# Down products of two SwiGLUs by Strassen's scheme, with the operands formed beside gate and up and kept in DRAM

## Chip, cores and metric

The kernel runs on one core of one Trainium2 chip. The metric is device time in microseconds (us) of one execution. The engines are TensorE (PE, with its weight loads PEld), VectorE (DVE), ScalarE (ACT), GpSimd (POOL) and SyncE (SP); SP and POOL here also issue the DMA transfers.

## What is computed

A decoder layer on x of 1024 positions by 1024 features, in float32. A SwiGLU (D_FF = 2816) stands ahead of the mixing block and another behind it:

```
def swiglu(x, w_gate, w_up, w_down):
    return (jax.nn.silu(x @ w_gate) * (x @ w_up)) @ w_down

x = x + 0.5 * swiglu(rms_norm(x, ffn1_norm), ffn1_w_gate, ffn1_w_up, ffn1_w_down)
# projection, sliding-window attention and chunkwise mLSTM, gated and merged: x = x + merged @ w_out
x = x + 0.5 * swiglu(rms_norm(x, ffn2_norm), ffn2_w_gate, ffn2_w_up, ffn2_w_down)
return rms_norm(x, final_norm)
```

## The kernel before

Features lie on the 128 partitions, positions on the free axis, in two halves of 512 (`HALVES`). A float32 matmul is done as three matmuls of type float32r: each operand is split into a high and a low part, and hi x hi, hi x lo and lo x hi are summed in PSUM (`mm3`, L318 to L320). A split is one copy on ACT (`whi`, L77 or L337) and one subtraction on DVE (`wlo`, L89 or L338; L337 and L338 are `parted`, which also splits moving operands).

**Gate and up** (`gate_up`) already use Strassen's scheme (Winograd's form: 7 products and 15 sums for a 2 x 2 of blocks). The blocks are halves of the features, halves of the positions, and pairs of row tiles s and s + 11. `PRODUCTS` is the order 1, 2, 6, 7, 4, 5, 3; a product is done for gate and for up (w = 0, 1), each a `group` of 12 matmuls (L421) into one PSUM bank. Product 2 accumulates in product 1's bank, products 7 and 4 in product 6's, product 3 in product 5's; DVE adds the rest (L447 for products 6 and 7, L451 for 4, 5 and 3). The first `LEAD` = 4 pairs do products 1 and 2 ahead, while DVE still prepares the operands of the others (`mixed`); after that a round takes all 7, in the first three pairs the 5 that are left. `gated` forms silu(gate) * up with one tanh on ACT (L429) and two operations on DVE (L432, L433) and writes the result to DRAM, `gd`, with the pair's row and half. Weights are split three products ahead (`prepare`, `split`), and sums of weights are formed in place (`sum_of`, L411).

**Down** (`ffn`) is a plain product: six chunks of row tiles (`CHUNKS`: 2, then 4 each). `fetch` loads the results of a chunk back from `gd` (L534) through the ring `nsq` of 24 tiles and splits them into one of three slots; `tail` starts the first three while gate and up finish. `down` does, for an output tile d and a half, the matmuls of a chunk in one bank, and DVE adds a quarter of it to the residual tile (L567). Residual tiles X are loaded as the stage begins (`loadx`). In the last chunk each finished tile goes to `done`: in the first SwiGLU it is written out, and when the first half is complete its norm is formed (`norm`: L264 sums of squares, L307 on DVE, L308 on ACT, L310 on POOL) while PE does the other half; in the second SwiGLU the final norm is formed (`final`), the end in `QUARTERS`.

Each engine takes its instructions in the order in which the program issues them; the schedule is written by hand. `bg` holds generators, and `pump` advances each by one step behind every group. A tile that is allocated anew waits for the last use of its buffer.

## Time and profile before

| | |
|---|---|
| median of 3 runs | 2519.94 us (2517.06 to 2520.85) |
| the profiled execution | 2524.41 us, of which its span is 2522.6 |
| mean granted TensorE clock | 0.978 of full speed |
| first SwiGLU: gate and up, down | about 20 to 467 us, 467 to 720 |
| mixing | about 720 to 1810 us |
| second SwiGLU: gate and up, down | about 1810 to 2251 us, 2251 to 2510 |

Times in the rows are counted from the span's start. A busy time is the union of an engine's instructions; the granted clock (PEclk) is a share of TensorE's full 2.4 GHz, and 0.5 is its other level. A line of waits says which instruction kept an engine idle until it ended; L447 or L567 there is a line of the kernel.

### The profile page before, as it was taken

What the parts mean: (1) busy time and instruction counts of PE and PEld (TensorE: products, weight loads), DVE (VectorE), ACT (ScalarE), POOL (GpSimd) and SP (SyncE); (2) the same over time, 40 slices, a digit from 0 to 9 for tenths busy, and PEclk for the clock granted to TensorE, in tenths of its full rate; (3) what the DMA queues carried; (4) which work ended last, traced back from release to release, by engine and by line L of the source; (5) the groups of instructions that cost most, each with busy time, mean ns of one, the idle gap of its engine ahead of it and who ended that gap; (6) DMA issues with size and microseconds to landing.
All of it is one profiled execution on the core that took longest, in us unless ns stands there. A gap on an engine that the chain in (4) does not pass through costs nothing.

```text
span 2522.6 us, 29816 instructions
## 1 busy us (share of the span) xinstructions
PE 2418.4 (96%) x11370; PEld 2004.2 (79%) x11370; DVE 1557.2 (62%) x2520; ACT 874.9 (35%) x1546; POOL 241.0 (10%) x210
## 2 busy tenths in 40 slices
PE   7899999899998999999999999999889999999997
PEld 6788888688887878888777788888668888878886
DVE  6876666554468864555658944445687666665535
ACT  4323223321136642333346623332432223231203
POOL 0000000000034330000233400000000000000002
PEclk8999999999999999999999999999889999999998
DMA  4322221542241212222531122223523222245322
GB/s 171 103 84 92 75 84 63 191 143 84 76 135 59 72 61 87 77 86 84 173 104 56 49 86 86 74 82 126 170 72 105 88 88 77 78 140 159 111 59 92
DMA packets 115183, 246.08 MB, mean 98 GB/s; under 512 B 10976, under 2 KB 18272, under 8 KB 115040
## 3 DMA queue, kind: packets, MB, share of 16 engines
q1 hardware_dynamic: 112976, 243.18, 30.0%
q8 instruction: 90, 1.47, 0.2%
q0 software_dynamic: 1200, 0.79, 0.2%
q14 instruction: 53, 0.43, 0.1%
q10 hardware_dynamic: 864, 0.21, 0.0%
HBM read 207.69 MB, written 36.44 MB: 97 GB/s over the span
## 4 chain that ended last, share of the span: by engine, by line
PE 77%; DVE 14%; ACT 3%; DMA 2%; issue 2%; SPq 0%; DVEq 0%; POOL 0%; ACTq 0%
PE mm L421 30%; PE mm L318 13%; PE mm L319 13%; PE mm L320 13%; DVE P L973 1%; PE mm L834 1%; DVE PT L1012 1%; PE mm L835 1%; PE mm L836 1%; DVE wlo L89 1%; DVE P L993 1%; DVE nsq L264 1%; PE lm L1114 1%; DMA nsq<-xd 1%; PE lm L1142 1%
## 5 line engine op out<-in xcount | busy, mean ns | idle before, releaser
L318 PE MATMUL mm<-s,whi 128*128 128x512 f32 (+1 forms) x1776 | 705.4, 397 | 16.3 <-DVE nsq L567 15.4
L320 PE MATMUL mm<-s,wlo 128*128 128x512 f32 (+1 forms) x1776 | 695.6, 392 | 1.7 <-POOL wlo L89 1.5
L421 PE MATMUL mm<-s,whi 128*128 128x512 f32 x2112 | 664.6, 396 | 33.9 <-DVE nsq L447 13.3
L319 PE MATMUL mm<-s,whi 128*128 128x512 f32 (+1 forms) x1776 | 694.9, 391 | 0.0
L421 PEld LDWEIGHTS mm<-s,whi 128*128 128x128 f32 x2112 | 403.0, 191 | 123.1 <-DVE nsq L447 14.2
L421 PE MATMUL mm<-s,wlo 128*128 128x512 f32 x1056 | 416.4, 394 | 0.0
L318 PEld LDWEIGHTS mm<-s,whi 128*128 128x128 f32 x1776 | 338.2, 190 | 87.2 <-ACT whi L77 13.7
L320 PEld LDWEIGHTS mm<-s,wlo 128*128 128x128 f32 x1776 | 337.7, 190 | 74.8 <-POOL wlo L89 3.2
L319 PEld LDWEIGHTS mm<-s,whi 128*128 128x128 f32 x1776 | 338.4, 191 | 64.7
L77 ACT ACTIVATE whi<-wraw 128x1024 fp32r<-128x1024 f32 (+2 forms) x210 | 215.0, 1029 | 234.1 <-PE mm L319 109.6
L89 DVE TENSOR_TENSOR wlo<-wraw,whi 128x1024 fp32r<-128x1024 f32 (+2 forms) x188 | 227.0, 1207 | 68.9 <-ACT whi L77 68.5
L567 DVE SCALAR_TENSOR_TENSOR nsq<-mm,nsq 128x512 f32<-128x512 f32 (+1 forms) x196 | 131.5, 678 | 201.7 <-PE mm L320 169.7
L421 PEld LDWEIGHTS mm<-s,wlo 128*128 128x128 f32 x1056 | 201.9, 191 | 43.1 <-DVE wlo L338 0.8
L337 ACT ACTIVATE whi<-wr 128x1024 fp32r<-128x1024 f32 x110 | 116.2, 1058 | 208.2 <-PE mm L421 155.1
L338 DVE TENSOR_TENSOR wlo<-wr,whi 128x1024 fp32r<-128x1024 f32 x110 | 134.3, 1222 | 53.3 <-ACT whi L337 53.2
L337 ACT ACTIVATE s<-nsq 128x512 fp32r<-128x512 f32 x112 | 67.9, 626 | 170.0 <-DMA nsq<-gd 155.3
L451 DVE TENSOR_TENSOR nsq<-mm,nsq 128x512 f32<-128x512 f32 x132 | 90.9, 688 | 56.3 <-PE mm L421 55.7
L89 POOL TENSOR_TENSOR wlo<-wraw,whi 128x1024 fp32r<-128x1024 f32 x22 | 52.7, 2400 | 708.5 <-ACT whi L77 708.5
L447 DVE TENSOR_TENSOR nsq<-mm,nsq 128x512 f32<-128x512 f32 x88 | 60.6, 690 | 96.0 <-PE mm L421 96.0
L429 ACT ACTIVATE nsq<-nsq 128x512 f32<-128x512 f32 x66 | 41.8, 633 | 192.2 <-DVE nsq L451 190.2
L421 PE MATMUL mm<-nsq,whi 128*128 128x512 f32 x352 | 108.4, 389 | 0.0
L338 DVE TENSOR_TENSOR s<-nsq,s 128x512 fp32r<-128x512 f32 x112 | 76.0, 688 | 45.7 <-ACT s L337 45.4
(250 smaller groups left out, 2732.9 us busy)
## 6 DMA issues: line engine op xcount, KB each, us to landing
wraw<-win SPq DMA_DIRECT2D x84, 512.0 KB, 3.6
wr<-gu SPq DMA_DIRECT2D x74, 512.0 KB, 4.1
wraw<-dn SPq DMA_DIRECT2D x48, 512.0 KB, 3.8
...
```

The source lines that it names most:

```text
L77: self.nc.scalar.activation(hv, v, AF.Copy)
L89: (self.nc.gpsimd if self.on_pool else self.nc.vector).tensor_sub(lv, v, hv.bitcast(F32))
L318: nc.tensor.matmul(ps, hi, xh, start=first, stop=False)
L319: nc.tensor.matmul(ps, hi, xl, start=False, stop=False)
L320: nc.tensor.matmul(ps, lo, xh, start=False, stop=last)
L337: nc.scalar.activation(hi, x, AF.Copy)
L338: nc.vector.tensor_sub(lo, x, hi.bitcast(F32))
L421: nc.tensor.matmul(ps, a[:, k], op[p](k, x), start=first and k == 0 and j == 0, stop=k == 3 and j == 2, skip_group_check=not first)
L429: nc.scalar.activation(st["th"], z[0], AF.Tanh, scale=0.5)
L447: nc.vector.tensor_add(t, ps, st[s, "s1", w])
L451: nc.vector.tensor_add(z, ps, z)
L567: nc.vector.scalar_tensor_tensor(x, ps, 0.25, x, op0=OP.mult, op1=OP.add)
```

## The change

Down becomes 7 products too. The row tiles are three chunks of pairs (`DOWN`: 4, 4 and 3 pairs f and f + 11), the outputs are pairs d, d + 1 (dp = 0 to 3), the blocks of the other factor are its halves by row and by position. A step is one product of one chunk: 4 banks (dp), in each 3 matmuls per pair.

The operands of the products are sums of the four results of a pair. `paired` forms them behind the pair's last product, splits each, and writes 7 x 2 tiles to `gd` in DRAM; for the first four pairs one result is parked in DRAM (`gx`) until then. `fetch` loads a product's operands, both parts, by one transfer on POOL's queue into one of two buffers in slot 1. The weights of a chunk are loaded by four transfers (`load`) into slot 0 or 2, summed in place and split two units a step.

In gate and up each product has its own PSUM bank, apart from 2 and 3; what 7 and 4 took from the bank is added on DVE (L458 and L461 in the order below). Products 1 and 2 of the next pair stand on both sides of product 3. The factor 0.25 of the down product goes into `gated`, where a `tensor_mul` becomes a `scalar_tensor_tensor`. The slots of the mixing part are exchanged, and the final norm counts d in another order. Cut to its core:

```diff
-CHUNKS = [(0, FT % CHUNK)] + [(f, CHUNK) for f in range(FT % CHUNK, FT, CHUNK)]
+DOWN = ((0, 4), (4, 4), (8, 3))
...
         def product(s, p, w, first):
-            key = {1: "A", 2: "A", 6: "C", 7: "C", 4: "C", 5: "B", 3: "B"}[p]
+            key = {2: 1, 3: 5}.get(p, p)
...
-                nc.vector.tensor_mul(th, th, z[1])
-                nc.sync.dma_start(gd[s + S2 * m, :, half * HS:(half + 1) * HS], th)
+                nc.vector.scalar_tensor_tensor(t, t, 0.25, z[1], op0=OP.mult, op1=OP.mult)
+                if (m, half) == (0, 0) and s < LEAD:
+                    nc.sync.dma_start(gx[s], st.pop(("g", s, 0, 0)))
+
+        def paired(s):
+            if s < LEAD:
+                st["g", s, 0, 0] = t = temp(pool)
+                nc.sync.dma_start(t, gx[s])
+            (a, b), (c, d) = ([st.pop(("g", s, m, h)) for h in range(2)] for m in range(2))
+            f = nc.vector.tensor_sub
+            for p, x, sub in ((3, d, (f, d, d, b)), (2, c, (f, b, b, a)), (1, a, (nc.vector.tensor_add, a, a, d)),
+                              (7, d, (f, c, c, a)), (5, b, None), (6, a, None), (4, c, None)):
+                part = [temp(pool, R32) for _ in range(2)]
+                parted(x, *part)
+                for i in range(2):
+                    nc.sync.dma_start(gd[PRODUCTS.index(p), s, :, i], part[i].bitcast(F32))
+                yield
+                if sub:
+                    sub[0](*sub[1:])
+                    yield
...
-                key, m, half = {4: ("s1", 1, 0), 5: ("u7", 1, 1), 3: ("u6", 0, 1)}[p]
-                z = st[s, key, w]
-                nc.vector.tensor_add(z, ps, z)
+                key, to, m, half = {4: (7, 1, 1, 0), 5: (7, 7, 1, 1), 3: (6, 6, 0, 1)}[p]
+                nc.vector.tensor_add(st[s, to, w], ps, st[s, key, w])
...
+                if p == 3 and w:
+                    bg.append(paired(s))
...
+        def load(c, i):
+            s0, a = DOWN[c]
+            flat = slot(i, [16 * HS], F32)
+            for m in range(2):
+                for h in range(2):
+                    t = flat[:, (2 * m + h) * 4 * a * 128:][:, :4 * a * 128]
+                    f = FT // 2 * h + s0
+                    nc.sync.dma_start(t.rearrange("p (d x) -> p d x", d=4),
+                                      I[f"dn{n}"][m::2, :, f:f + a].rearrange("d p f c -> p d (f c)"))
+                    raw[c, m, h] = t
+
+        def fetch(i):
+            if i < len(steps):
+                c, p = steps[i]
+                s0, a = DOWN[c]
+                t = moving["buf"][:, i % 2, :a]
+                nc.gpsimd.dma_start(t, gd[PRODUCTS.index(p), s0:s0 + a].rearrange("s p i t -> p s i t"))
+                moving[i] = t
...
         def tail(p):
+            if p == 2:
+                load(0, 0)
+            elif p == 7:
+                moving["buf"] = slot(1, [2, 4, 2, HS])
+                fetch(0)
+                fetch(1)
             elif p == 5:
+                load(1, 2)
...
+        for i, (c, p) in enumerate(steps):
+            if i:
+                fetch(i + 1)
+            if i == 2:
+                for d in range(0, KT, 2):
+                    loadx(d, 1)
+            elif i in (3, 4):
+                for d in range(1, KT, 2):
+                    loadx(d, i - 3)
+            if (c, p) == (1, 1):
+                load(2, 0)
...
+            for span in spans:
+                for dp in range(4):
+                    cols = slice(span[0] % HS, span[0] % HS + span[1])
+                    ps = times(i, moving[i], dp, cols)
+                    if dp % 2 == 0 and span[0] != QUARTERS[1][0]:
+                        t = prepare()
+                    elif dp % 2 and t:
+                        sum_of(*t)
+                        t = None
+                    add = nc.vector.tensor_add
+                    if p == 1:
+                        u[dp] = temp(pool)
+                        nc.scalar.activation(u[dp], ps, AF.Copy)
+                    elif p in (6, 7):
+                        if p == 7:
+                            add(X[2 * dp][1], X[2 * dp][1], u[dp])
+                        add(u[dp], ps, u[dp])
+                    else:
+                        d, h = {2: (0, 0), 4: (1, 0), 5: (1, 1), 3: (0, 1)}[p]
+                        x = X[2 * dp + d][h]
+                        if p in (4, 5):
+                            add(x, x, u[dp])
+                        add(x[:, cols], ps, x[:, cols])
+                        if end:
+                            done(2 * dp + d, span)
+                    pump()
...
-    gd = dram.tile([FT, 128, S], F32, name="gd")
+    gd = dram.tile([len(PRODUCTS), FT // 2, 128, 2, HS], F32, name="gd")
```

Three places in the instruction order. The first is DVE in the early part of the first SwiGLU's gate and up, at the adds of products 6 and 7 of pair 0 (`mm_664` and the like are PSUM banks, `wlo_678` the low half of the weights for product 4). Before:

```order
L338 TENSOR_TENSOR wlo_678<-wr_288,whi_677 128x1024
L447 TENSOR_TENSOR nsq_681<-mm_664,nsq_305 128x512
L447 TENSOR_TENSOR nsq_710<-mm_695,nsq_320 128x512
L198 TENSOR_SCALAR bhalf_712<-binf_685 128x42
L205 CAST identr_714<-ident_74 128x128
L206 TENSOR_SCALAR lmask_716<-nsq_683 128x128
L338 TENSOR_TENSOR wlo_734<-wr_389,whi_733 128x1024
L447 TENSOR_TENSOR nsq_737<-mm_664,nsq_305 128x512
```

And of the changed kernel:

```order
L328 TENSOR_TENSOR wlo_679<-wr_289,whi_678 128x1024
L458 TENSOR_TENSOR nsq_682<-mm_665,nsq_306 128x512
L458 TENSOR_TENSOR nsq_711<-mm_696,nsq_321 128x512
L188 TENSOR_SCALAR bhalf_713<-binf_686 128x42
L195 CAST identr_715<-ident_74 128x128
L196 TENSOR_SCALAR lmask_717<-nsq_684 128x128
L328 TENSOR_TENSOR wlo_736<-wr_390,whi_735 128x1024
L458 TENSOR_TENSOR nsq_739<-mm_722,nsq_682 128x512
```

No row moved; the last one, the add of product 7, reads a bank of its own (`mm_722`), where it read product 6's (`mm_664`).

The second is DVE in a long round, from product 6 to the first add of product 4 or, in the changed kernel, of product 7. Before:

```order
L338 TENSOR_TENSOR wlo<-wr,whi 128x1024
L447 TENSOR_TENSOR nsq<-mm,nsq 128x512 x2
L338 TENSOR_TENSOR wlo<-wr,whi 128x1024
L447 TENSOR_TENSOR nsq<-mm,nsq 128x512 x2
L338 TENSOR_TENSOR wlo<-wraw,whi 128x1024
L451 TENSOR_TENSOR nsq<-mm,nsq 128x512
```

And of the changed kernel, where L444 is a sum and L328 with `nsq` a split of `paired`:

```order
L458 TENSOR_TENSOR nsq<-mm,nsq 128x512
L444 TENSOR_TENSOR nsq<-nsq 128x512
L458 TENSOR_TENSOR nsq<-mm,nsq 128x512
L328 TENSOR_TENSOR nsq<-nsq 128x512
L328 TENSOR_TENSOR wlo<-wraw,whi 128x1024
L458 TENSOR_TENSOR nsq<-mm,nsq 128x512
L444 TENSOR_TENSOR nsq<-nsq 128x512
```

Between the adds of a product there now stands one operation of `paired` for each group.

The third is POOL from the early constants to the norm ahead of the mixing part, which holds the whole first down stage. Before:

```order
L182 IOTA nsq 128x256
L274 TENSOR_TENSOR nv<-nv,mhalf 128x4
L310 TENSOR_TENSOR s_4584<-nsq,s_4584 128x512 x8
L689 MEMSET hist 128x24
L691 MEMSET C 128x1040
```

And of the changed kernel:

```order
L172 IOTA nsq 128x256
L564 DMA s_3554<-gd 128x4x1024 x14
L564 DMA s_3554<-gd 128x3x1024 x7
L264 TENSOR_TENSOR nv<-nv,mhalf 128x4
L300 TENSOR_TENSOR s_4799<-nsq,s_4799 128x512 x8
```

The 21 fetches of the down stage are POOL's only work there, ahead of the norm's.

## Rows read from the trace of the kernel before

**Rows 1.** The page: span, TensorE's busy time, its granted clock by slices, one group.

```profile
span 2522.6 us, 29816 instructions
PE 2418.4 (96%) x11370; PEld 2004.2 (79%) x11370; DVE 1557.2 (62%) x2520; ACT 874.9 (35%) x1546; POOL 241.0 (10%) x210
...
PEclk8999999999999999999999999999889999999998
...
L318 PE MATMUL mm<-s,whi 128*128 128x512 f32 (+1 forms) x1776 | 705.4, 397 | 16.3 <-DVE nsq L567 15.4
```

**Rows 2.** Busy times by stretch (first row: columns): inside gate and up, inside down.

```profile
core 0: us, PE busy (x) PEld busy (x) DVE busy (x) ACT busy (x) POOL busy (x), PEclk, DMA share, GB/s
200.00:300.00 100.00, 100.00 (x443) 82.81 (x442) 62.33 (x74) 29.01 (x34) 0.00 (x0) 1.00 0.26 85
300.00:400.00 100.00, 100.00 (x443) 82.81 (x442) 67.51 (x80) 29.87 (x36) 0.00 (x0) 1.00 0.25 82
...
520.00:660.00 140.00, 140.00 (x619) 115.93 (x618) 67.93 (x93) 28.67 (x39) 0.00 (x0) 1.00 0.30 92
```

**Rows 3.** The same by stretch: both early gate-and-up parts, both starts of down.

```profile
85.00:120.00 35.00, 28.33 (x118) 22.96 (x117) 30.96 (x56) 8.68 (x11) 0.34 (x1) 0.90 0.37 114
1870.00:1900.00 30.00, 23.32 (x91) 18.75 (x91) 23.68 (x31) 5.51 (x6) 0.00 (x0) 0.83 0.30 101
467.00:505.00 38.00, 28.90 (x118) 22.70 (x117) 21.24 (x32) 11.95 (x19) 0.00 (x0) 0.91 0.74 236
2251.00:2290.00 39.00, 32.67 (x132) 26.12 (x131) 22.97 (x35) 13.06 (x19) 0.00 (x0) 0.91 0.74 246
```

**Rows 4.** What PE waited for, whole span: us in total, times, longest.

```profile
PE mm L318 <- DVE nsq L567: 15.4, 5, 6.7
PE mm L421 <- DVE nsq L447: 13.3, 2, 6.7
```

**Rows 5.** Groups of instructions by line and shape: busy us, mean ns, idle before.

```profile
L338 DVE TENSOR_TENSOR wlo<-wr,whi 128x1024 fp32r<-128x1024 f32 x110 | 134.3, 1222 | 53.3 <-ACT whi L337 53.2
...
L451 DVE TENSOR_TENSOR nsq<-mm,nsq 128x512 f32<-128x512 f32 x132 | 90.9, 688 | 56.3 <-PE mm L421 55.7
L338 DVE TENSOR_TENSOR s<-nsq,s 128x512 fp32r<-128x512 f32 x112 | 76.0, 688 | 45.7 <-ACT s L337 45.4
...
L337 ACT ACTIVATE s<-nsq 128x512 fp32r<-128x512 f32 x112 | 67.9, 626 | 170.0 <-DMA nsq<-gd 155.3 <-DVE nsq L1368 11.0 <-DVE nsq L346 2.3
```

**Rows 6.** DMA from 10 to 20 us, SyncE's queue alone, loads at full share.

```profile
DMA packets 2130, 3.97 MB, mean 397 GB/s; under 512 B 191, under 2 KB 191, under 8 KB 2130
```

**Rows 7.** Lines L1192 and L1225, the transfers on POOL's queue (ns of issue).

```profile
L1192 POOL DMA_DIRECT2D s<-kh x2: 778/790/803, 1266.2 to 1355.5; - x2
...
DMA to landing us min/median/max: 3.4/3.7/4.0
...
L1225 POOL DMA_DIRECT2D VS<-vh x1: 766/766/766, 1265.5 to 1265.5; - x1
```

**Rows 8.** DMA: queue share from 1355 to 1361 us; GB/s from 1356.8 to 1358.6.

```profile
q0 software_dynamic: 528, 0.26, 24.1%
...
GB/s 0 0 0 0 46 23 46 23 23 68 114 148 148 148 159 171 239 216 296 319 330 330 319 341 353 319 319 319 273 250 171 103 68 68 46 23 11 0 0 0
```

**Rows 9.** Order of time, end of the first SwiGLU: start us, us, engine and line.

```profile
697.95 0.69 DVE L264 TENSOR_TENSOR nsq<-nsq 128x512 f32<-128x512 f32 x1 [0.70 <-ACT nsq L262]
...
717.60 5.92 POOL L310 TENSOR_TENSOR s<-nsq,s 128x512 fp32r<-128x512 f32 x4 [2.27 <-ACT s L308]
```

**Rows 10.** What PE waited for from 2480 to 2523 us, the longest.

```profile
PE mm L271 <- DVE nsq L264: 5.2, 1, 5.2
```

**Rows 11.** Busy times at the first two issues on POOL's queue, columns as above.

```profile
1265.50:1266.50 1.00, 1.00 (x10) 1.00 (x10) 0.00 (x0) 0.00 (x0) 1.00 (x2) 1.00 0.33 131
1355.50:1356.50 1.00, 1.00 (x7) 1.00 (x6) 0.93 (x6) 0.59 (x1) 0.79 (x2) 0.50 0.06 16
```

More of the change, by code (lines that the diff above doesn't have):

```diff
@@ L23 @@
 FT = 2816 // 128
-CHUNK = 4
 HALVES = ((0, HS), (HS, HS))
@@ L465, in behind @@
                     load(s + 1 if p == 2 else s + 2, 0, 0)
-        ahead = set(range(LEAD))
+        early = set(range(LEAD))
         for h in range(2):
@@ L480, in gate_up @@
             load(3, 0, h)
-        ahead.clear()
+        early.clear()
         yield
@@ new lines, in times @@
+        def times(i, t, dp, c):
+            key = (dp, {2: 1, 3: 5}.get(steps[i][1], steps[i][1]))
+            first = steps[i][1] not in (2, 3)
+            if first:
+                bank[key] = psum.tile([128, HS], F32, name="mm")
+            ps = bank[key][:, c]
+            hi, lo = (x[:, dp % 2] for x in parts[2 * i + dp // 2])
+            a = hi.shape[1]
+            for f in range(a):
+                for q, (wt, x) in enumerate(((hi, 0), (hi, 1), (lo, 0))):
+                    nc.tensor.matmul(ps, wt[:, f], t[:, f, x, c], start=first and f == 0 and q == 0,
+                                     stop=f == a - 1 and q == 2, skip_group_check=not first)
+            return ps
@@ L1444, in done2 @@
         else:
-            stats(pool, fa[h][:, own], x, d == 0)
+            stats(pool, fa[h][:, own], x, first)
             fa[p] = [fa[h][:, own]]
```

192 lines of the change are left out of this document (82 added, 110 removed).

## The prediction

> **What bounds the kernel now.** I read the page's first two parts, then busy times by stretch. TensorE is busy 96% of the span and its granted clock is at the full level nearly everywhere [rows 1]. Inside gate and up, and inside the down products, PE is 100% busy at clock 1.00, and neither VectorE (62 to 68% and 49%) nor ScalarE limits it [rows 2]. So a stage costs its matmuls times their pitch: 100 us for 443 matmuls and 140 us for 619 [rows 2], 0.226 us for one of 512 columns (the 397 ns that one of them lasts [rows 1] overlap its neighbours). Then I looked where PE stops. Two places in each SwiGLU matter here. At the start of the down products, 38 us hold 118 matmuls (26.7 us at that pitch) and 39 us hold 132 (29.8): 11.3 + 9.2 = 20.5 us are lost, to L567, whose residual tile and operand come late from DRAM, and to the lower clock behind the pause [rows 3, 4]. And in the early part of gate and up, product 7 stops 6.7 us for the add of product 6 (L447), which still has to read the PSUM bank into which 7 accumulates, and stands in VectorE's queue behind the preparation of the operands; 118 matmuls in 35 us and 91 in 30 lose 8.3 and 9.4 us there [rows 3, 4].
>
> **The change part by part.** All sums are against the profiled execution's 2524.4 us (span 2522.6 and 1.8 around it); it lies 4.5 us above the median 2519.9, so 4.5 come off at the end.
>
> (a) *Fewer matmuls.* Down had 22 row tiles x 8 x 2 halves x 3 = 1056 matmuls a SwiGLU, now 7 products x 4 x 11 x 3 = 924. 2 x 132 x 0.226 = **-59.7 us**, all on the path.
>
> (b) *Start of the down products.* Before, fetch and residual tiles were asked for when the stage began. Now the first weights go out after product 2 of the last round, two fetches after its product 7, i.e. three products of 24 x 0.226 = 5.4 us ahead: 16.3 us for 2 x 2.1 MB, and the second is needed 10.9 us later still. Residual tiles are needed only at the second product. I leave 1 us a SwiGLU for the seam: **-18.5 us** (bounds -20.5 and -10).
>
> (c) *Own PSUM banks.* Product 7 no longer waits for L447. What is late next is its neighbour's weight: the low half for product 4 stands one row ahead of those adds in VectorE's queue, and VectorE, behind by some 8 us there, gets to it when PE has finished 7. So 1 to 2 us of each stop stay, and since PE then runs ahead of a VectorE that has more to do (d), part comes back later. Of 17.7 us I take **-7 us** (bounds -15 and 0).
>
> (d) *Operands formed beside gate and up.* A round of 7 products is 168 matmuls, 38.0 us; VectorE is busy 62.3 + 67.5 us in 200, so 24.7 in a round [rows 2]. `paired` adds 7 splits and 4 sums of 512 columns, 11 x 0.69 = 7.6 us [rows 5]: 32.3 of 38.0, 85%, still hidden. ScalarE gets 7 x 0.63 = 4.4 on some 11. The first three rounds have 5 products, 27.1 us; VectorE has 5 weight splits (6.1), 4 sums (4.9), 10 evictions (6.9), 6 gatings (4.1) and the 7.6: 29.6 us by single durations, a tenth less back to back. It falls behind by 0 to 2.5 us a round, against weights split three products (16 us) ahead. If every split also waits for ScalarE as L338 did (45.7 us over 112, 0.41 each [rows 5]), the long rounds come to 32.3 + 14 x 0.41 = 38.0, no loss, and the short ones to 29.6 + 12 x 0.41 = 34.5, 7.4 late each: 44 us in both SwiGLUs. A VectorE that is behind finds ScalarE done, so I stay near the low end: **+4 us** (0 to 44). Writing 7 x 2 x 0.26 = 3.7 MB a round instead of 1.0 gives some 152 GB/s with the weights, where 397 was moved at full load [rows 6].
>
> (e) *Fetching the operands.* The operands were split after loading; now both halves come from DRAM: 21 fetches, 2.1 MB each (1.57 in the last chunk), through GpSimd's queue, each into the buffer that the product before last leaves. So a fetch has one product's time: 48 x 0.226 = 10.9 us (8.1 in the last chunk). Its nearest row is the 256 KB that GpSimd's queue moves into `s` (kh): 3.4 us alone [rows 7], with its packets at 319 to 353 GB/s on the plateau [rows 8]. At 335, 2.6 us are fixed and 2.1 MB take 6.3: 8.9 of 10.9, hidden; in the last chunk 7.3 of 8.1. Not hidden where SyncE's queue moves as much at once: the second chunk's weights (4.2 MB, asked for 5 us before the stage), 14 writes of the last round's operands and 16 residual tiles fall on steps 1 to 4, the third chunk's weights on 7 and 8; in the first SwiGLU the results go out during three steps of the last chunk. With both queues at 366 GB/s in all (between 335 and 397 [rows 6, 8]), a fetch beside 2.1 MB takes 2.6 + 11.5 = 14.1, 3.3 late; beside 1.05 MB 0.4 late: 3 x 3.3 + 3 x 0.4 = 11.1 a SwiGLU, and 3 x 1.7 = 5.1 in that last chunk. **+27 us** (17 at 397, 40 at 335).
>
> A rule to weigh here: the Trainium skill (DMA: Bandwidth & Descriptors, Anatomy of one DMA) fits a GpSimd-issued transfer with 2.0 us plus its bytes at 436 GB/s, an estimate of 6.8 us for 2.1 MB; the trace's 256 KB took 3.4 us where that fit gives 2.6, so it does not quite agree and the row decides. By the page's figure (e) would be about 4 us and the time 2453.
>
> (f) *Seam to the mixing part.* The first half of the residual was final 8 groups of 12 matmuls (21.7 us) before PE ended; now two steps, 16.3 us. Its norm is a chain from VectorE's last sum (at 697.95) to GpSimd's last low half (717.60 + 5.92), four of them 5.9 us [rows 9]: 25 us, of which PE now covers 5.4 less and VectorE's two adds per tile in products 4 and 5 delay the start: **+7 us** (2 to 12).
>
> (g) *End.* Before, PE waited 5.2 us there for the sums of squares [rows 10]. Now VectorE has two adds where it had one in products 4 and 5 (8 x 0.69 = 5.5 us more): **+3 us** (0 to 8). VectorE's weight splits and evictions in the down products (per step 2.4 + 1.4 + 3.5 = 7.3 of 10.9 us) cost nothing while PE and the fetch take longer.
>
> Sum: -59.7 - 18.5 - 7 + 4 + 27 + 7 + 3 = -44.2; 2524.4 - 44.2 = 2480.2, less 4.5: **2476 us**.
>
> **The rivals.** *All hidden* (the fetches cost 5 at most, the stops of (c) go by 13, the seam costs 5, end and (d) 2 each): -59.7 - 18.5 - 13 + 2 + 5 + 5 + 2 = -77.2, 2443. For it: SyncE's queue alone reached 397 GB/s; against: some 20 MB are wanted in the first 54 us of the stage, which is nearly that rate throughout. *The fetch is slow throughout* (the other side): it converts to another type on the way, and over its whole share, 24.1% of 6 us [rows 8], the 256 KB moved at 181 GB/s. At 181 a fetch takes 2.6 + 11.6 = 14.2 us, 3.3 late in 13 steps and 3.2 in 7: 65 us a SwiGLU, 131 in place of the 27: 2524.4 - 44.2 - 27 + 131 = 2584, 2580 by the median. It decides from where the 40 steps eat 71 us, 1.8 us each, a landing at 12.7 us or 208 GB/s. Against it stands the plateau, with packets of only 512 bytes. *VectorE bounds gate and up*: (d) at 44 and (c) at 0, 2523, no change. *GpSimd cannot write descriptors while VectorE works*: then every fetch starts an instruction (1.2 us) later, hidden in the plain steps, 1.2 more in the 15 contested ones: 18 us, 2494. Against: one issue took 0.77 us with VectorE idle and one 0.80 with it 93% busy [rows 7, 11]. The Trainium skill (SBUF — State Buffer, Who interferes with whom) states such a lockout for VectorE's two-port modes and excepts tensor_tensor, and the two issues agree. That the change does not drop the matmuls is excluded by the instruction order, which holds 924 of them a SwiGLU (those of 256 columns counted as halves).
>
> **How the numbers follow.** Forecast 0.54 (its own range 2455 to 2500), all hidden 0.25, slow fetch 0.10, VectorE-bound 0.08, lockout 0.03. The range leaves out the slow fetch and the worst of VectorE: 2440 to 2518. About 0.2% (5 us) is what a measurement of this kernel can tell from no change. Faster: 0.54 + 0.25 + 0.03 and a quarter of VectorE-bound, 0.84; same 0.04; slower 0.12.
>
> **What would show it.** PE's count in the down stage 7/8 of before; no wait of PE for the add of product 6; PE's waits inside the down products named to GpSimd's queue and lying at steps 1 to 4 and 7 to 8 alone (forecast), nowhere (all hidden), or in each step with about 3 us (slow fetch); median landing of a fetch 9 to 10 us, or 7, or 14. VectorE over 95% busy in gate and up with PE under 100% would be the VectorE case. I am wrong above all if the landing time of 2.1 MB is not what 256 KB let one expect.

## The result and the profile after

The changed kernel takes 2482.30 us (median of 4 runs, 2477.79 to 2483.14), the kernel before 2520.39 (4 runs, 2517.06 to 2522.57): a ratio of 0.9846 with a 95% interval of 0.9829 to 0.9863. The forecast was 2476 us with a range of 2440 to 2518. The profiled execution took 2482.01 us, its span is 2479.4: 43.2 us less than the span before, where the sum of the prediction said 44.2. By stage, from the first and last matmul of each (us):

| stage | before | after | difference |
|---|---|---|---|
| ahead of the first matmul of gate and up | 19.7 | 19.4 | -0.3 |
| gate and up, first SwiGLU | 447.4 | 453.5 | +6.1 |
| down, first, up to the first matmul of mixing | 252.4 | 229.4 | -23.0 |
| mixing | 1092.6 | 1087.8 | -4.8 |
| gate and up, second | 438.9 | 437.5 | -1.4 |
| down, second, and the end | 271.6 | 251.8 | -19.8 |

The total is close, the stages less so: the first gate and up became slower, and mixing, in which the forecast counted nothing but its seam, became faster.

The page of the changed kernel (L626 is now the matmul of down, L413 that of gate and up, L461 and L458 VectorE's sums from PSUM in gate and up, L564 the fetch):

```profile
span 2479.4 us, 30117 instructions
...
PE 2365.1 (95%) x11094; PEld 1956.3 (79%) x11094; DVE 1740.1 (70%) x2780; ACT 944.0 (38%) x1664; POOL 258.0 (10%) x246
...
s<-gd POOLq DMA_DIRECT2D x28, 2048.0 KB, 9.3
...
s<-gd POOLq DMA_DIRECT2D x14, 1536.0 KB, 6.9
```

TensorE has 53 us less work than in [rows 1] and VectorE 183 us more. The last figures of the DMA rows are the medians from issue to landing of a fetch: 9.3 and 6.9 us, where 8.9 and 7.3 were forecast. The rival of the slow fetch (14.2 us) falls with these two rows.

Busy times by stretch, columns as in [rows 2]:

```profile
85.00:120.00 35.00, 29.64 (x120) 24.05 (x119) 31.57 (x57) 9.27 (x12) 0.35 (x1) 0.90 0.43 133
...
200.00:300.00 100.00, 100.00 (x443) 82.84 (x442) 82.03 (x106) 38.36 (x54) 0.00 (x0) 1.00 0.51 166
300.00:400.00 100.00, 100.00 (x443) 82.84 (x442) 81.83 (x107) 38.64 (x54) 0.00 (x0) 1.00 0.44 144
...
460.00:500.00 40.00, 34.70 (x139) 27.81 (x138) 30.30 (x38) 14.36 (x21) 1.48 (x2) 0.92 1.08 394
1860.00:1900.00 40.00, 36.67 (x155) 29.89 (x155) 35.86 (x47) 14.14 (x18) 0.00 (x0) 0.96 0.33 112
```

In the long rounds VectorE went from 62 to 68 up to 82 us in 100, TensorE still never stops there, and the writes of the operands brought 144 to 166 GB/s (152 with the weights were forecast). From 460 us the DMA queues are full: 394 GB/s.

What TensorE waited for in the whole span (total, times, longest), and the places in order of time (start, duration; in brackets the wait ahead of it):

```profile
PE mm L261 <- DVE nsq L254: 21.5, 7, 5.3
PE mm L413 <- DVE nsq L461: 15.9, 6, 5.4
PE mm L626 <- DMA s<-gd: 12.8, 6, 3.3
```

```profile
109.79 0.77 PE L413 MATMUL mm<-nsq,whi 128*128 128x512 f32 x1 [5.36 <-DVE nsq L461]
...
465.74 0.70 PE L413 MATMUL mm<-nsq,whi 128*128 128x512 f32 x2 [3.11 <-DVE nsq L461]
...
497.00 1.11 PE L626 MATMUL mm<-s,whi 128*128 128x512 f32 x2 [2.19 <-DMA s<-gd]
...
558.23 0.87 PE L626 MATMUL mm<-s,whi 128*128 128x512 f32 x2 [3.03 <-DMA s<-gd]
...
682.81 1.44 PE L261 MATMUL mm<-mean,nsq 128*128 128x2 f32 x6 [3.72 <-DVE nsq L254]
...
2252.81 0.80 PE L626 MATMUL mm<-s,whi 128*128 128x512 f32 x1 [3.29 <-DMA s<-gd]
```

The wait for the residual tile (L567 in [rows 4]) is gone: the first down matmul follows the last of gate and up without a pause. The wait of product 7 for product 6's sum (L447) is gone too, but L461 stands in its place. A matmul whose moving operand is `nsq` belongs to product 3, and product 3 accumulates in product 5's bank, which L461 reads. The waits for an operand number three in each SwiGLU; by the count of matmuls they stand at the start of steps 3, 5 and 8 both times.

To weigh the terms I counted, from the starts of successive matmuls in the timeline, how much later than the pitch (0.2267 us per 512 columns) each came; this takes in the lower clock behind a stop. That lateness, before and after:

| place | before | after | term, forecast | term, by lateness |
|---|---|---|---|---|
| (a) 2 x 132 matmuls fewer | | | -59.7 | -59.8 |
| (b) start of down | 11.6 + 9.4 | 0 | -18.5 | -21.0 |
| (c) early stop in gate and up | 9.0 + 9.9 | 8.0 + 5.2 | -7 | -5.7 |
| (d) stops at 169, 466, 1927, 2222 us | 0 | 2.2 + 5.2 + 1.1 + 1.6 | +4 | +10.1 |
| (e) waits for an operand | 0 | 10.9 + 9.0 | +27 | +19.9 |
| (f) seam to mixing | 0.3 | 7.2 | +7 | +6.9 |
| (g) half and quarter norms, end | 8.6 + 11.6 | 6.4 + 11.5 + 11.9 | +3 | +9.6 |
| mixing | | | 0 | -4.8 |
| sum | | | -44.2 | -44.8 |

The remaining 1.6 us to the measured 43.2 lie in places below what this count resolves. The sum was right because errors of both signs met: (d) and (g) came out 6 us higher each, (e) and mixing 7 and 5 lower. That it came within 1 us is in part luck. So the experiments ask after the terms one by one.

### The profile page after: what moved, and what is told of

Read it like the earlier page. It is cut to its first block, busy times and chain, and to the rows that moved or that the text cites. A ratio compares the mean times of both kernels' runs of the same rounds, so it can differ in the third digit from the quotient of the medians.

```text
span 2479.4 us, 30117 instructions
## 1 busy us (share of the span) xinstructions
PE 2365.1 (95%) x11094; PEld 1956.3 (79%) x11094; DVE 1740.1 (70%) x2780; ACT 944.0 (38%) x1664; POOL 258.0 (10%) x246
## 4 chain that ended last, share of the span: by engine, by line
PE 51%; DVE 12%; DMA 3%; ACT 3%; issue 3%; SPq 0%; DVEq 0%; POOL 0%; ACTq 0%; POOLq 0%
PE mm L413 14%; PE mm L308 7%; PE mm L310 7%; PE mm L309 7%; PE mm L626 5%; DMA gd<-nsq 2%; DVE P L1042 1%; PE mm L903 1%; DVE PT L1081 1%; PE mm L904 1%; PE mm L905 1%; DMA s<-gd 1%; DVE P L1062 1%; DVE wlo L87 1%; PE lm L1183 1%
## 5 line engine op out<-in xcount | busy, mean ns | idle before, releaser
L413 PE MATMUL mm<-s,whi 128*128 128x512 f32 x2112 | 659.6, 393 | 19.7 <-ACT nsq L452 9.4
L413 PEld LDWEIGHTS mm<-s,whi 128*128 128x128 f32 x2112 | 400.0, 190 | 107.1 <-ACT nsq L452 11.1
L308 PE MATMUL mm<-s,whi 128*128 128x512 f32 x1056 | 423.5, 401 | 0.9 <-DVE s L1368 0.9
L310 PE MATMUL mm<-s,wlo 128*128 128x512 f32 x1056 | 415.4, 393 | 1.5 <-POOL wlo L87 1.5
L309 PE MATMUL mm<-s,whi 128*128 128x512 f32 x1056 | 414.6, 393 | 0.0
L413 PE MATMUL mm<-s,wlo 128*128 128x512 f32 x1056 | 414.2, 392 | 0.0
L626 PE MATMUL mm<-s,whi 128*128 128x512 f32 (+1 forms) x1256 | 391.4, 394 | 15.3 <-DMA s<-gd 12.8
L626 PEld LDWEIGHTS mm<-s,whi 128*128 128x128 f32 x1256 | 239.8, 193 | 66.5 <-DMA s<-gd 6.3
L626 PE MATMUL mm<-s,wlo 128*128 128x512 f32 (+1 forms) x628 | 246.2, 392 | 0.0
L413 PEld LDWEIGHTS mm<-s,wlo 128*128 128x128 f32 x1056 | 200.4, 190 | 42.7 <-DVE wlo L328 0.8
L87 DVE TENSOR_TENSOR wlo<-wraw,whi 128x1024 fp32r<-128x1024 f32 (+1 forms) x138 | 171.5, 1243 | 69.6 <-ACT whi L75 69.1
L75 ACT ACTIVATE whi<-wraw 128x1024 fp32r<-128x1024 f32 (+1 forms) x154 | 159.7, 1042 | 74.1 <-PE mm L310 23.7
L327 ACT ACTIVATE whi<-wr 128x1024 fp32r<-128x1024 f32 (+1 forms) x122 | 128.0, 1050 | 156.3 <-PE mm L413 92.8
L328 DVE TENSOR_TENSOR wlo<-wr,whi 128x1024 fp32r<-128x1024 f32 (+1 forms) x122 | 147.6, 1212 | 36.4 <-ACT whi L327 34.7
L327 ACT ACTIVATE whi<-s 128x1024 fp32r<-128x1024 f32 (+1 forms) x72 | 71.0, 986 | 238.2 <-PE mm L626 230.4
L564 POOL DMA_DIRECT2D s<-gd x42 | 31.8, 756 | 1188.5 <-DMA s<-dn 783.4
L626 PEld LDWEIGHTS mm<-s,wlo 128*128 128x128 f32 x628 | 121.1, 193 | 24.3
L328 DVE TENSOR_TENSOR nsq<-nsq 128x512 fp32r<-128x512 f32 x162 | 110.6, 686 | 31.6 <-ACT nsq L327 29.0
L413 PE MATMUL mm<-nsq,whi 128*128 128x512 f32 x352 | 113.3, 404 | 15.9 <-DVE nsq L461 15.9
## 6 DMA issues: line engine op xcount, KB each, us to landing
s<-dn SPq DMA_DIRECT2D x16, 1024.0 KB, 11.2
```

The source lines that it names most:

```text
L75: self.nc.scalar.activation(hv, v, AF.Copy)
L87: (self.nc.gpsimd if self.on_pool else self.nc.vector).tensor_sub(lv, v, hv.bitcast(F32))
L308: nc.tensor.matmul(ps, hi, xh, start=first, stop=False)
L309: nc.tensor.matmul(ps, hi, xl, start=False, stop=False)
L310: nc.tensor.matmul(ps, lo, xh, start=False, stop=last)
L327: nc.scalar.activation(hi, x, AF.Copy)
```

## The experiments

All runs in one table. Times in us; the ratio is that to the kernel before on the same chip, with its 95% interval; the stages are those of the profiled execution.

| run | median | ratio | gate/up 1 | down 1 | mixing | gate/up 2 | down 2, end |
|---|---|---|---|---|---|---|---|
| changed kernel | 2482.30 | 0.9846 (0.9829-0.9863) | 453.5 | 229.4 | 1087.8 | 437.5 | 251.8 |
| e1_nopair | 2471.08 | 0.9807 (0.9794-0.9821) | 446.2 | 232.5 | 1088.5 | 434.3 | 249.0 |
| e2_spread | 2482.04 | 0.9847 (0.9827-0.9866) | 454.7 | 232.4 | 1088.9 | 436.4 | 252.1 |
| e3_stats | 2477.88 | 0.9832 (0.9816-0.9848) | 453.6 | 225.9 | 1088.4 | 437.2 | 250.8 |
| e4_shared | 2495.53 | 0.9909 (0.9893-0.9924) | 457.9 | 234.7 | 1086.7 | 444.6 | 251.3 |
| e5_paced | 2469.76 | 0.9796 (0.9783-0.9810) | 450.5 | 224.7 | 1089.4 | 435.6 | 247.9 |
| e6_pool | 2480.70 | 0.9844 (0.9830-0.9857) | 454.4 | 231.8 | 1088.2 | 439.0 | 250.3 |
| e7_shared_nopair | 2480.92 | 0.9842 (0.9828-0.9856) | 447.0 | 235.8 | 1086.2 | 439.0 | 253.5 |
| e8_stats2 | 2475.68 | 0.9826 (0.9812-0.9840) | 448.1 | 224.3 | 1095.1 | 438.0 | 248.8 |
| e9_own3 | 2460.03 | 0.9755 (0.9742-0.9769) | 438.1 | 230.6 | 1086.2 | 430.1 | 252.3 |
| e10_all | 2449.07 | 0.9714 (0.9701-0.9727) | 440.4 | 221.0 | 1095.0 | 429.5 | 240.8 |
| e11_latefetch | 2479.55 | 0.9838 (0.9823-0.9852) | 448.8 | 228.5 | 1088.7 | 436.1 | 253.2 |
| e12_latefetch2 | 2512.36 | 0.9965 (0.9952-0.9977) | 450.2 | 250.3 | 1088.6 | 436.2 | 266.9 |

How far apart must two runs be? The gate and up of e2, e3, e5, e8, e11 and e12 is the changed kernel's, and its first one took 448.1 to 454.7 us in those profiles, mainly since the stop near 462 us lasted anything from 1.1 to 5.4 us; the first 20 us of the stage make up to 2.5 us more. The stop's length goes with what VectorE itself waited for transfers just ahead of it: 1.3 us in e8 (stop 1.1), 3.4 in the changed kernel (3.1), 5.6 in e2 (5.4). So a difference of 3 us between two medians says little, and where one matters I go by the stage.

### The added work on VectorE (e1_nopair)

```diff
-                part = [temp(pool, R32) for _ in range(2)]
-                parted(x, *part)
                 for i in range(2):
-                    nc.sync.dma_start(gd[PRODUCTS.index(p), s, :, i], part[i].bitcast(F32))
+                    nc.sync.dma_start(gd[PRODUCTS.index(p), s, :, i], x)
                 yield
                 if sub:
-                    sub[0](*sub[1:])
                     yield
```

> Left out: the splits and sums of paired (7 copies on ScalarE, 7 subtractions and 4 sums on VectorE in a round); the 14 writes to gd a round stay, of unsplit values. Compared with the changed kernel (2482.3 us, ratio 0.985). Theory 1, VectorE's queue: the stops of TensorE that are new there (at 160, 460, 1920 and 2220 us; matmuls start 2.2 + 5.2 + 1.1 + 1.6 = 10.1 us late against the pitch) go with the work: 2472 us, VectorE in 200 to 300 us back from 82 to about 62 busy. Term (d) of the prediction: 4 us, 2478. Rival, the DMA queue: the stops at the stage's end (460 and 2220) come from transfers that are late there, the 6.8 us of them stay: 2479.

11.2 us less. The stage that answers is the right one: gate and up lost 7.3 + 3.2 us. Busy times of this run in the long rounds, and its waits of TensorE for that sum (L458 in its numbering):

```profile
200.00:300.00 100.00, 100.00 (x443) 82.81 (x442) 64.71 (x75) 28.57 (x34) 0.00 (x0) 1.00 0.54 173
```

```profile
PE mm L413 <- DVE nsq L458: 8.5, 2, 5.4
```

Two of the six stops are left, those at 110 and 1866 us; the four new ones are gone although the writes stayed. So (d) comes from the added work, and is about 10 us, not 4. At the stop of 169 us VectorE is busy without a pause, 9.96 of the 10 us from 160 on. For the two at the stage's end (466 and 2222 us) its queue is not the whole: in the changed kernel VectorE itself waits for transfers just ahead of the first, from 450 to 467 us:

```profile
DVE nsq L328 <- DMA gd<-nsq: 1.8, 1, 1.8
DVE s L575 <- DMA s<-dn: 1.6, 1, 1.6
```

The first is a buffer that a write of an operand still holds, the second the down weights. In e1 there is no such wait: the buffers of the split operands and ScalarE's seven copies went with the edit. So e1 does not part VectorE's work from the full DMA queue there.

### Shared banks, with and without that work (e4_shared, e7_shared_nopair)

```diff
-            key = {2: 1, 3: 5}.get(p, p)
+            key = {2: 1, 7: 6, 4: 6, 3: 5}.get(p, p)
...
-            ps = product(s, p, w, p not in (2, 3))
+            ps = product(s, p, w, p in (1, 6, 5))
...
-                nc.vector.tensor_add(t, ps, st[s, {6: 1, 7: 6}[p], w])
+                nc.vector.tensor_add(t, ps, st[s, 1, w])
...
-                key, to, m, half = {4: (7, 1, 1, 0), 5: (7, 7, 1, 1), 3: (6, 6, 0, 1)}[p]
+                key, to, m, half = {4: (1, 1, 1, 0), 5: (7, 7, 1, 1), 3: (6, 6, 0, 1)}[p]
```

> Only the PSUM banks of gate and up are undone: products 7 and 4 accumulate in product 6's bank, as in the kernel before. Compared with the changed kernel (2482.3 us). Theory 1, a stop that moved: TensorE stops again at product 7 for 6.7 us and no longer at product 3 for 5.4 and 3.3; lateness 9.0 + 9.9 in place of 8.0 + 5.2, 5.7 us: 2488. Term (c) of the prediction: 7 us, 2489; its bounds 2482 and 2497. Rival: VectorE alone sets the pace there and the bank changes nothing: 2482.

13.2 us more, twice the forecast of (c) and near its bound; the gate-and-up stages account for 4.4 + 7.1 = 11.5, and at the first seam mixing's first matmul waits 6.5 us, once. The same edit on top of e1's:

> Shared PSUM banks in gate and up, and the splits and sums of paired left out (both edits together: with the work, shared banks cost 13.2 us, 2495.5 against 2482.3). Compared with the kernel without that work and with own banks (2471.1 us). Theory 1, the two work together: without the added work VectorE is behind only once in each gate and up, as in the kernel before, and shared banks cost what the stops there differ by, 5.7 us: 2477, with no stop at 153, 183 and 1952. Rival: shared banks cost the same with and without: 2484.

By the median 9.8 us more than e1, by the gate-and-up stages 0.8 + 4.7 = 5.5; the rest lies at the seam (the same 6.5 us; why they come in these two runs is not known) and in the second down stage, whose program the edit leaves alone. TensorE's waits for product 6's sum in e4 and in e7:

```profile
PE mm L413 <- DVE nsq L458: 20.2, 6, 6.5
```

```profile
PE mm L413 <- DVE nsq L455: 13.2, 2, 6.7
```

Without the added work there are two such stops, as in [rows 4]; with it six, in later rounds too. So terms (c) and (d) are no two numbers: own banks are worth 5.5 us alone and 11.5 once VectorE has the additional work.

### A bank for product 3 (e9_own3)

```diff
-            key = {2: 1, 3: 5}.get(p, p)
+            key = {2: 1}.get(p, p)
...
-            ps = product(s, p, w, p not in (2, 3))
+            ps = product(s, p, w, p != 2)
...
                 nc.vector.tensor_add(st[s, to, w], ps, st[s, key, w])
+                if p == 5:
+                    nc.vector.tensor_add(st[s, 6, w], ps, st[s, 6, w])
```

> Product 3 of gate and up gets a PSUM bank of its own too; VectorE adds product 5 once more (2 x 0.69 us a round). All six stops of TensorE that are left in the changed kernel's gate and up behind 100 us wait for the add of product 5 (L461), which reads the bank into which 3 accumulates one group later; matmuls start 8.0 + 2.2 + 5.2 + 5.2 + 1.1 + 1.6 = 23.3 us late there. Compared with the changed kernel (2482.3 us). Theory 1, the shared bank: VectorE may be late by a group only there, and by three products (16 us) elsewhere, so nearly all stops go: 2462. Rival, VectorE's backlog itself: the stops move to the next product or weight, as from product 7 to 3 in the change, or grow with the added sums: 2478 or more.

22.3 us less; gate and up 15.4 + 7.4 = 22.8. TensorE's longest waits in this run, and its long rounds:

```profile
PE mm L261 <- DVE nsq L254: 17.6, 6, 5.3
PE mm L628 <- DMA s<-gd: 15.1, 8, 3.7
PE mm L413 <- ACT nsq L452: 9.2, 4, 4.4
```

```profile
200.00:300.00 100.00, 100.00 (x443) 82.80 (x442) 89.58 (x120) 39.46 (x56) 0.00 (x0) 1.00 0.51 168
```

No wait for VectorE's sum is left in gate and up, with VectorE busier than before, 89.6 us in 100. The stops had been in other rounds, though: in pairs 0 and 2 and in the last pair, where product 3 follows product 5 at once. In the long rounds product 1 of the next pair stands between them. In the short rounds, from 120 to 190 us, the changed kernel and e9:

```profile
120.00:190.00 70.00, 68.28 (x301) 56.24 (x300) 65.33 (x87) 24.68 (x34) 0.00 (x0) 1.00 0.57 192
```

```profile
120.00:190.00 70.00, 70.00 (x311) 57.96 (x310) 66.76 (x92) 25.07 (x35) 0.00 (x0) 1.00 0.57 192
```

In pair 2 the sum of product 5 ended 4.3 us after the last matmul that it needs in the changed kernel, and TensorE stopped; in e9 it ended 9.9 us after, and TensorE went on. This settles what the stops were: not too much work on VectorE, but a place where TensorE tolerated a lateness of one group (12 matmuls, 2.7 us). The change had moved that place from product 7 to product 3; it had not taken it away.

### That work on GpSimd (e6_pool)

```diff
-                parted(x, *part)
+                nc.scalar.activation(part[0], x, AF.Copy)
+                nc.gpsimd.tensor_sub(part[1], x, part[0].bitcast(F32))
...
-            f = nc.vector.tensor_sub
+            f = nc.gpsimd.tensor_sub
-            for p, x, sub in ((3, d, (f, d, d, b)), (2, c, (f, b, b, a)), (1, a, (nc.vector.tensor_add, a, a, d)),
+            for p, x, sub in ((3, d, (f, d, d, b)), (2, c, (f, b, b, a)), (1, a, (nc.gpsimd.tensor_add, a, a, d)),
```

> The 7 subtractions and 4 sums of paired go from VectorE to GpSimd, which is idle there (11 x 1.5 us by the 1.52 us that one of this size takes there in the norm, 16.7 of a round's 27 to 38). Compared with the changed kernel (2482.3 us). Theory 1, VectorE's queue: as without that work (2471.1): stops at 160, 460, 1920 and 2220 go, 2471. Rival, both engines hold each other up when they work at once: VectorE's 688 ns and GpSimd's 1.52 us grow, and less than half is won: 2477 or more. Rival, the longer way through GpSimd holds the ring of temporaries and the first fetches: 2482.

No gain (1.6 us by the median, gate and up 0.9 + 1.5 longer); theory 1 falls. VectorE's groups in the changed kernel, and below them in e6 (busy us, mean ns of one):

```profile
L461 DVE TENSOR_TENSOR nsq<-mm,nsq 128x512 f32<-128x512 f32 x132 | 90.6, 687 | 38.7 <-PE mm L413 38.6
...
L425 DVE SCALAR_TENSOR_TENSOR nsq<-nsq 128x512 f32<-128x512 f32 x66 | 45.7, 692 | 2.3
...
L403 DVE TENSOR_TENSOR wraw<-wraw,wr 128x1024 f32<-128x1024 f32 x22 | 26.8, 1219 | 0.0
```

```profile
L462 DVE TENSOR_TENSOR nsq<-mm,nsq 128x512 f32<-128x512 f32 x132 | 90.2, 687 | 62.3 <-PE mm L413 62.0
...
L425 DVE SCALAR_TENSOR_TENSOR nsq<-nsq 128x512 f32<-128x512 f32 x66 | 70.1, 1062 | 2.3
...
L403 DVE TENSOR_TENSOR wraw<-wraw,wr 128x1024 f32<-128x1024 f32 x22 | 42.2, 1916 | 0.0
```

VectorE's operations whose inputs both lie in SBUF became up to 1.6 times as long beside GpSimd's; those that read PSUM kept their 687 ns. That this ate the gain is the likely reading; the theory of the ring is not excluded, for ScalarE's splits of the operands still waited 22.4 us for writes to free a buffer (18.1 in the changed kernel). The Trainium skill (SBUF — State Buffer, Who interferes with whom) says that a VectorE instruction with two SBUF inputs contends with a GpSimd instruction that reads SBUF, and one with at most one SBUF input, outside the modes that use two ports, does not; these rows agree with it.

### Transfers put off (e2_spread, e5_paced)

In e2 the later weights are loaded in quarters, at the top of four steps each:

```diff
-            elif p == 5:
-                load(1, 2)
...
-            if (c, p) == (1, 1):
-                load(2, 0)
+            if 2 <= i <= 5:
+                load(1, 2, i - 2)
+            if 8 <= i <= 11:
+                load(2, 0, i - 8)
```

> The weights of the second chunk of down are loaded by quarters at steps 3 to 6 and those of the third at steps 9 to 12, in place of four quarters at once 5 us ahead of the stage and at step 8. Compared with the changed kernel (2482.3 us). Theory 1, contention: the six waits for an operand (12.8 us, with the lower clock behind them matmuls start 10.9 + 9.0 = 19.9 us late) go: 2462 us, no wait of PE for s<-gd. By the prediction's price of term (e), 27 us: 2455. Rival: a fetch is as long as a step by itself, or waits for its buffer: 2482 with the same waits.

Nothing gained, and the waits are no less:

```profile
PE mm L629 <- DMA s<-gd: 14.6, 5, 4.5
```

The reason is in SyncE's own rows. In the changed kernel and in e2 (issue time, time of the group):

```profile
470.53 3.79 SPq L555 DMA_DIRECT2D s<-dn  x4
...
535.60 5.34 SPq L555 DMA_DIRECT2D s<-dn  x4
```

```profile
499.91 0.46 SPq L560 DMA_DIRECT2D s<-dn  x1
...
511.74 0.38 SPq L560 DMA_DIRECT2D s<-dn  x1
...
520.77 22.20 SPq L560 DMA_DIRECT2D s<-dn  x6
```

Step 9 begins after 570 us (the fetch at its top goes out at 571.3 us in the changed kernel), and yet all eight quarters are out by 543: SyncE waits here only for buffers. A place in the program paces nothing there. The second chunk's quarters did go out later, from 500 us in place of 470, behind residual tiles. With that the first SwiGLU's wait at step 3 went, and the one at step 5 grew from 1.6 to 4.5 us. In e5 the quarters stand on GpSimd's queue, behind a fetch that has to wait until TensorE leaves its buffer:

```diff
+            for k in {3: (0,), 4: (1, 2), 5: (3,)}.get(i, ()):
+                load(1, 2, k)
+            if 8 <= i <= 11:
+                load(2, 0, i - 8)
...
-                    nc.sync.dma_start(t.rearrange("p (d x) -> p d x", d=4),
+                    (nc.gpsimd if c else nc.sync).dma_start(t.rearrange("p (d x) -> p d x", d=4),
```

> Down's weights of the second and third chunk stand on GpSimd's queue behind a fetch (quarters at steps 4, 5, 5, 6 and 9 to 12), where the fetch's wait for its buffer keeps pace with TensorE; on SyncE's queue the same order by steps had paced nothing (they went out at 500 to 543 us, as soon as their buffers were free, and the waits for an operand stayed, 14.6 us). Compared with the changed kernel (2482.3 us). Theory 1, contention: a step now asks for 2.1 + 1.05 MB, 289 GB/s in 10.9 us; the waits of 12.8 us (19.9 us late with the clock) shrink to those of the first steps beside the residual tiles, below 5: 2467. Rival: the whole stretch from 440 to 560 us is at the queue's limit (391 GB/s were moved), what is put off is missing later: 2480. Rival: the transfers on one queue serve each other in turn and every fetch comes late: above 2490.

12.5 us less. GpSimd's rows, and what is left of the waits:

```profile
502.66 0.74 POOL L569 DMA_DIRECT2D s<-gd  x1 [10.27 <-PE mm L629]
503.39 0.76 POOL L560 DMA_DIRECT2D s<-dn  x1
513.54 0.74 POOL L569 DMA_DIRECT2D s<-gd  x1 [9.39 <-PE mm L629]
514.27 1.52 POOL L560 DMA_DIRECT2D s<-dn  x2
```

```profile
PE mm L629 <- DMA s<-gd: 7.8, 3, 3.8
```

The down stages lost 4.7 + 3.9 us, and gate and up 4.9, half of it in the first 20 us of the first stage, which the edit leaves alone. The waits fell from 12.8 to 7.8, above the forecast of under 5: three remain in the first steps (3 and 5), beside the residual tiles. The fetches of 440 to 560 us, in the changed kernel and in e5 (KB, median from issue to landing):

```profile
s<-gd POOLq DMA_DIRECT2D x9, 2048.0 KB, 12.1
```

```profile
s<-gd POOLq DMA_DIRECT2D x9, 2048.0 KB, 10.4
```

A fetch by itself takes 8.8 us, less than the 10.9 of a step. So contention is the cause of the 5 us of waits that went. That the rest is contention too, and there to stay, is argued: the stretch from 440 to 560 us moved 342 GB/s on average, of some 400 that the queues reach.

### The early fetch (e11_latefetch, e12_latefetch2)

```diff
                 moving["buf"] = slot(1, [2, 4, 2, HS])
-                fetch(0)
-                fetch(1)
...
+        fetch(0)
         for i, (c, p) in enumerate(steps):
-            if i:
-                fetch(i + 1)
+            fetch(i + 1)
```

> Only the first two operand fetches of down are asked for when the stage begins, as the kernel before did, not in the last round of gate and up. Compared with the changed kernel (2482.3 us). Theory 1, term (b): the early fetch is what took the late starts away (matmuls 11.6 + 9.4 = 21 us late in the kernel before): TensorE waits some 9 to 17 us for the first operand in each SwiGLU, the landing of one fetch alone and of the first one in the changed kernel: 2500 to 2520. Rival: the queue is full from 440 us on either way, and the fetch that starts later meets fewer writes and weights, so that later waits for operands (12.8 us) go in turn: 2490 or less.

2479.6, no difference, and this too tested nothing: the fetches went out at 450.4 us as ever, since GpSimd had nothing to wait for. In e12 it has:

```diff
+            elif p == 3:
+                x = st[FT // 2 - 1, 6, 1][:, :4]
+                v = pool.tile([128, 4], F32, name="nv", bufs=1)
+                nc.gpsimd.tensor_sub(v, x, x)
+                fetch(0)
+                fetch(1)
```

> The first two operand fetches of down now really go out when the stage begins: GpSimd first does a subtraction of 4 columns that needs the last sum of gate and up (in the run before, moved to the same place in the program without such a need, they went out at 450.4 us, 22 us ahead of the stage as in the changed kernel, at 452.1). Compared with the changed kernel (2482.3 us) and that run (2479.6). Theory 1, term (b): TensorE waits for the first operand in each SwiGLU as long as a fetch takes, 9 to 16 us, 18 to 32 in all, and the waits behind it (12.8 us, 19.9 with the clock) shrink by some, since the weights land first: 2492 to 2512. The prediction's figure for the early start is 18.5: 2501. Rival: what the early fetch wins, it loses again in the queue that is full until 560 us: 2485 or less.

30.1 us more, at the upper end of theory 1. GpSimd's rows and TensorE's waits for an operand:

```profile
472.18 0.69 POOL L604 TENSOR_TENSOR nv<-nsq 128x4 f32<-128x4 f32 x1 [382.73 <-DVE nsq L461]
472.92 1.71 POOL L564 DMA_DIRECT2D s<-gd  x2
```

```profile
PE mm L630 <- DMA s<-gd: 44.8, 7, 16.6
```

Two waits of 16.6 us; the others stay. Fetching early is worth 30 us in the new scheme, more than the 21 which the late start of the old one had cost.

### The matmuls of the norms (e3_stats, e8_stats2)

```diff
-        for _ in range(3):
+        for _ in range(7 if which == 1 else 3):
             yield
...
-        for _ in range(0 if p == end else 2):
+        for _ in range(0 if p == end else 6):
```

> The matmuls that sum the squares for the norm ahead of mixing, and for the first half of the final norm, stand two groups of 9 matmuls later in TensorE's order (four more steps of their generators). Compared with the changed kernel (2482.3 us). Theory 1: the stops of 3.7 us at 682.8 and 2436.1 are only a matter of that place, since VectorE's last sum comes 3.7 us after TensorE gets there; 6.1 and 6.4 us with the clock go: 2470. Rival, the prediction's seam: the chain from the last sum to the norm sets the start of mixing, so what is won at 682.8 comes back at 702, and only the 6.4 of the second place go: 2476. If the chain of the final norm sets the end too: 2482.

In e8 the transposes behind the sums are moved as well:

```diff
-        for r in rstd_of(pool, psum, [acc]):
+        for r in rstd_of(pool, psum, [acc], gap=6 if which == 1 else 2):
...
-        for _ in range(0 if p == end else 2):
+        for _ in range(0 if p == end else 6 if p == HALVES[0] else 2):
             yield
-        for r in rstd_of(pool, psum, fa[p], p[1] // 128):
+        for r in rstd_of(pool, psum, fa[p], p[1] // 128, 6 if p == HALVES[0] else 2):
...
-        yield
-        yield
+        for _ in range(gap):
+            yield
```

> As the run that put the matmuls of the sums of squares two groups later, and now the transposes behind them two groups later too, and the first quarter of the final norm left where it was: there TensorE had stopped anew at the transposes for GpSimd's power (4.3 us at 688.6, 6.2 at 2443.5). Compared with the changed kernel (2482.3 us) and that run (2477.9). Theory 1, order alone: both stops of 3.7 us go with the clock behind them, 6.1 + 6.4: 2470. Rival, the norm's chain sets the seam: it starts later by as much, TensorE waits at 702 instead: 2476. Rival, none of it: 2482.

The medians are 4.4 and 6.6 us lower, but the stages tell less: down 1 and mixing together took 1317.2 us in the changed kernel, 1314.3 in e3 and 1319.4 in e8; down 2 with the end 251.8, 250.8 and 248.8. What TensorE waited for at the seam, from 660 to 710 us, in e3 and in e8:

```profile
PE mm L269 <- POOL nv L264: 4.3, 1, 4.3
PE mm L878 <- POOL s L300: 2.1, 2, 1.0
```

```profile
PE mm L878 <- POOL s L300: 3.5, 4, 1.0
```

Each time the stop is gone from its place and the time is not: mixing starts earlier and waits for the norm's low halves. The rival, that the chain sets the seam, is right at the first place; at the second 1 to 3 us were won, of the 6.4 expected.

### Together (e10_all)

It holds e9's and e5's edits and e8's, with `12 if p == HALVES[0]` for the transposes of the second SwiGLU.

> Together: product 3's own bank, the later weights of down on GpSimd's queue behind the fetches, and the matmuls and transposes of the norms two groups later (in the second SwiGLU the transposes five groups). Alone the second gave 12.5 us and the third 6.6 against the changed kernel (2482.3). Theory 1, each at its own place: 2482.3 - 12.5 - 6.6 - 20 = 2443 with the bank's 20, 2463 if the bank gives nothing. Rival: what is won ahead of the down products comes back in them, since the transfers of 440 to 560 us take as long: 2455 with the bank at 20.

2449.07 us, 33.2 less than the changed kernel, a ratio of 0.9714 to the kernel before: between the 2443 of theory 1 and the 2455 of the rival, and faster than both kernels. Gate and up kept what the bank won (13.1 + 8.0), the down stages and mixing gave 12.2 together. Alone the three edits had given 22.3 + 12.5 + 6.6 = 41.4, so some 8 us do not add up.

## Why the prediction was right, and where it was not

**What bounds it**, (a): right. TensorE is 100% busy in the long rounds and the 264 matmuls came off one for one, -59.8 us.

**(b) Start of down**: right, -21.0 where -18.5 was taken; e12 shows that the early fetch does it.

**(c) Own banks**: the size was near (-5.7, forecast -7), but the step "what is late next is its neighbour's weight" failed. Late next was product 3, which the change leaves in product 5's bank; the diff says so in the line on `key`. e9 priced that remaining sharing at 22.3 us, more than any measured term but (a).

**(d) VectorE in gate and up**: mis-sized, 10.1 for 4, inside its bounds. The busy sum of a long round (32.3 of 38.0 us) was right: 82 us in 100 were measured for 85, and no stop lies in a long round. For the short rounds I had VectorE fall behind by 0 to 2.5 us each, against weights split three products (16 us) ahead. The step that failed is that slack: at the bank that product 3 shares with 5 it is one group, 2.7 us, and VectorE was 4.3 us late there in pair 2. In the last round VectorE's own waits for transfers add to it, for which I had nothing.

**(e) Contention**: the mechanism held, at steps 3, 5 and 8 where I had named 1 to 4 and 7 to 8, and the size did not: 19.9 us for 27. In the last chunk, for which I had 5.1, no wait came, and the nine fetches up to 560 us took a median of 12.1 us, where I had 14.1 beside 2.1 MB. The step that failed is the rate of both queues, 366 GB/s, taken between 335 and 397; the full queues move 354 to 412 here, and for 397 the prediction had said 17. From 440 to 560 us, in 40 slices:

```profile
GB/s 87 236 327 393 388 400 403 405 405 412 376 380 397 388 386 399 411 397 399 354 391 397 405 395 373 391 283 135 411 158 0 29 370 395 388 370 390 403 374 288
```

The 335 came from the 256 KB transfer of [rows 8], whose plateau was too short to show the rate. A fetch by itself, issued at 603.9 us, from 602 to 616:

```profile
GB/s 0 0 0 0 0 0 0 0 0 105 82 82 386 421 386 445 386 421 421 433 456 386 410 410 410 246 59 23 23 35 12 0 0 0 0 0 0 0 0 0
```

It moves at 386 to 456 GB/s and lands after 8.8 us (median of it and the next): the forecast 8.9 was right by a rate too low and a fixed part too small. The Trainium skill (DMA: Bandwidth & Descriptors, Anatomy of one DMA) has 436 GB/s for the rate, which agrees, and 2.0 us for the rest, which by 8.8 less 2.1 MB at 410 GB/s (5.1 us) is 3.7 here.

**(f) Seam**: right in size (+6.9 for +7), and e3 with e8 show that the norm's chain sets it, as the prediction said. Most of the loss stands earlier than I had it, at the sums of squares at 682.8 us and not ahead of mixing's first matmul.

**(g) End**: mis-sized, 9.6 for 3, beyond the bound of 8. I counted VectorE's two sums per tile at the very end and overlooked the matmuls of the first half's norm at 2436 us, which stop TensorE for 3.7 us in the midst of the last chunk (6.4 us with the clock). Two more waits, 2.5 us in all at 2451 and 2454 us, are for VectorE's sums (L669) ahead of matmuls of the last quarters.

**Mixing**: forecast as unchanged but for the seam, measured 4.8 us shorter, and in every run of a kernel that keeps the changed one's seam (1086.2 to 1089.4, against 1092.6). The whole part before and after:

```profile
719.50:1812.10 1092.60, 1052.54 (x5368) 876.69 (x5367) 660.09 (x1350) 463.03 (x998) 206.88 (x182) 0.98 0.28 89
```

```profile
702.30:1790.10 1087.80, 1049.84 (x5366) 874.02 (x5366) 662.54 (x1352) 463.45 (x999) 207.37 (x183) 0.99 0.29 89
```

The granted clock differs a little. By the trace's records it stood at the lower level for 33.7 us of this part before and for 29.9 after; a matmul of 512 columns starts every 0.43 us there and every 0.23 at the full level, so I estimate that the clock explains 1.8 of the 4.8 us. A shorter wait for a sum of squares (`nacc`, 2.2 us before and 1.1 after) explains 1.1 more, and the rest is spread over small places. Nor does the clock order the runs: e5 has 33.9 us at the lower level, as much as the kernel before, and its mixing is still 3.2 us shorter. Why mixing is shorter is not settled; no run was made for it.

**The rivals**: slow fetch, refuted by the landings. VectorE-bound gate and up, refuted by TensorE at 100% in the long rounds and 68.3 us of 70 in the short ones. Lockout: the 42 issues took 741 to 952 ns, so no start of an instruction was lost. All hidden: e10 comes to 2449, near its 2443, but only after three further edits.
